# A hybrid RWKV-7 and neighbourhood-attention trunk on one core: the first norm given priority, chunk products over one head's 64 rows, and a load buffer of its own for the decay exponents

## The chip, the cores and the metric

The kernel runs on one core of a Trainium2 chip. The metric is the device time of one execution in microseconds. A core has a matrix engine (PE, with its weight loads shown as PEld), a vector engine (DVE), a scalar engine (ACT), a general engine (POOL) and queues that issue DMAs; most loads here are issued by the queue SP, in order.

## The reference

Two layers are applied to 512 latent tokens and 128 prompt tokens of width 1024 in float32. Every sub-layer starts with a root-mean-square norm and a modulation (shift, scale, gate) made from the conditioning vector; layer 0 mixes tokens with a bidirectional delta-rule recurrence of 16 heads of 64, layer 1 with neighbourhood attention, and each is followed by a squared-ReLU MLP of width 4096. The recurrence is, per head and direction:

```
sa    = S @ (-kk_t)
S_new = S * w_t + sa (kk_t * a_t)^T + v_t k_t^T
y_t   = S_new @ r_t        # w_t = exp(-exp(-softplus(-z) - 0.5))
```

Outputs are both token streams, the final scan states of the prompt, and the prompt's attention keys and values.

## The kernel before, in words

The prompt and the latent tokens are one array of 640 columns, features on the 128 partitions. Instructions are placed by a list scheduler: it simulates a time line of all engines, and each engine then runs its own list in the fixed order that came out; a block under `high_priority` is preferred when several instructions are ready. Within the scan the order on PE is pinned by hand to the order of the program (`mm`).

*Front* (`start_norm`, `rms_bcast`). Four DMAs load the tokens, one the first low-rank weight (`w0[0]`), then 16 DMAs of 512 KB the modulation weights, through six buffers. ACT squares eight tiles (line 331), DVE adds them (336), PE sums over partitions (359), DVE takes an inverse root, five diagonal tiles and five products (381) spread it over the partitions, ACT copies it out, and DVE multiplies the eight token tiles (441). Each quarter of the modulation is produced by PE (286, 296) and added up by DVE (300); ACT then makes the normed tiles `hp` (454), and DVE the token differences `dl` (457 to 460). POOL multiplies `w0[0]` into `w0[1]` (478). The projections follow. Their weight buffers lie where the token tile was.

*Scan.* Tokens are cut into 5 tiles of 128 and these into chunks of 32; two directions run against each other. For each step of tiles, eight units (head group, direction, half) are prepared. `prep_elem` does the elementwise part, once for two units (a pair): it loads the decay exponents (`wi`, line 910, 128x520), `ld_d` (912) and `ld_s` (914), sums the exponents by a scan on DVE (916), takes two exponentials on ACT (917, 918), copies the end factors (`FC`, 920) and makes the scaled keys `KB` (932, 933) on POOL. Then for each unit it takes a free tile C, sets to zero the half of the rows that belongs to the other head, once by a memset on POOL (942) and once by an activation with scale 0 on ACT (939), and writes four scaled products (947, POOL). `prep_group` makes the chunk products of `KB` and C on PE (`pp`, 128 rows by 64 columns, 128 columns streamed): the rows that are not the head's are zero in C. The second 64 columns streamed are the identity kept in C. ACT copies the results (972, 974), and DVE masks one part back into C (977), into the half that held the zeros.

`invert` (984 to 998) solves a 32x32 triangular system for all chunks of a step by some 120 small instructions on DVE. `chain_step` then runs the recurrence over four pairs of chunks: state products (PE, `A`), `U` from the inverse (needs the inversion), the update of the state in bank `B` by 64x64 products at two positions of the array (`state_update`), and `Y`. Between its pieces `fill` prepares units of the next steps; `m_i` and `e_i` count how far the products and the elementwise part have come, and C tiles return to the list `free` after every second chunk. `GU` tiles take the values by DMA (1018). The first preparations run beside the V projection (`tm_product`, 239), whose 20 outputs call `fill` too.

Of the kernel before, what the change touches and what calls it, by code (L numbers as in the profile page):

```python
# [8 lines left out]
F32 = mybir.dt.float32  # L9
F32R = mybir.dt.float32r  # L10
I32 = mybir.dt.int32
AF = mybir.ActivationFunctionType
ALU = mybir.AluOpType
# [3 lines left out]
P = 128  # L17
# [4 lines left out]
T = TS + TP  # L22
# [150 lines left out]
class K:  # L173
# [152 lines left out]
    def rms_bcast(self, x, pool):  # L326
        nc = self.nc
        acc = None
        for k in range(KT):
            sq = pool.tile([P, T], F32, name="sq")  # L330
            nc.scalar.activation(sq, x[:, k, :], AF.Square)
            if acc is None:
                acc = sq
            else:
                n = pool.tile([P, T], F32, name="sqa")
                nc.vector.tensor_tensor(n, acc, sq, op=ALU.add)
                acc = n
        return self.rms_second(self.rms_first(acc, pool), pool)

    def ssq(self, k):  # L340

# [83 lines left out]
    def start_norm(self, st, hp, dl, w0):  # L425

        nc = self.nc
        p2 = self.pool(st, "n1", 2)
        adp = self.pool(st, "adp", 6)
        ps2 = self.pool(st, "n1p", 4, space=PSUM)  # L430
        xt = p2.tile([P, KT, T], F32, name="xt", bufs=1)
        xv = self.A["xT"].rearrange("(k p) t -> p k t", p=P)
        for k2 in range(4):
            nc.sync.dma_start(xt[:, 2 * k2:2 * k2 + 2, :], xv[:, 2 * k2:2 * k2 + 2, :])
        nc.sync.dma_start(w0[0], self.A["lora1"][0])
        self.ada_prepare(p2)
        nc.vector.memset(hp[:, :, 0:1], 0.0)
        nc.vector.memset(hp[:, :, T + 1:T + 2], 0.0)
        rb = self.rms_bcast(xt, p2)
        for k in range(KT):  # L440
            nc.vector.tensor_tensor(xt[:, k, :], xt[:, k, :], rb, op=ALU.mult)
        gs = self.const.tile([P, 8, 2], F32, name="gs00")
        m = self.mods[0]
        for j in range(4):
            for b in (4 + j, j):
                ps = ps2.tile([P, 512], F32, name="adp")
                self.ada_second(*self.ada_first(0, b, adp, ps[:, :256]), ps[:, 256:260])
            ks = slice(2 * j, 2 * j + 2)
            nc.vector.scalar_tensor_tensor(gs[:, ks], m[:, 8 + 2 * j:10 + 2 * j], 1.0,
                                           self.par("norm_g")[:, ks].unsqueeze(2).broadcast_to([P, 2, 2]),  # L450
                                           op0=ALU.add, op1=ALU.mult)
            for k in range(2 * j, 2 * j + 2):
                for a, c, i in ((0, TS, 0), (TS, TP, 1)):
                    nc.scalar.activation(hp[:, k, a + 1:a + 1 + c], xt[:, k, a:a + c], AF.Identity, scale=gs[:, k, i:i + 1],
                                         bias=m[:, k, i:i + 1])
                s = p2.tile([P, T], F32, name="n_s")
                nc.vector.tensor_tensor(s, hp[:, k, 0:T], hp[:, k, 2:T + 2], op=ALU.add)

                nc.vector.tensor_copy(s[:, TS - 1:TS + 1], hp[:, k, TS - 1:TS + 3:3])
                nc.vector.scalar_tensor_tensor(dl[:, k], s, 0.5, hp[:, k, 1:T + 1], op0=ALU.mult, op1=ALU.subtract)  # L460
# [266 lines left out]

    def c_slots(self, pool, n, par):

        for i in range(n):  # L730
            c = pool.tile([P, 26, 64], F32, name=f"C{i}")
            self.nc.any.tensor_copy(c[:, 16:18, :].rearrange("p a x -> p (a x)"), self.cst("ident"))
            self.free[par].append(c)

    def scan_pools(self, st):
# [147 lines left out]
    def fill(self, n):  # L883

        for i in range(n + 1):
# [8 lines left out]
            if self.m_g == 2:  # L894
                self.m_g = 0
                self.m_i += 1
                if self.m_i % 8 == 0:
                    self.invert(u[0])

    def prep_elem(self, ts, hg, d, i):  # L900

        nc = self.nc
        if "FC" not in ts:
            ts["FC"] = self.fcp.tile([P, 2, 2, 2, 4], F32, name="FC")
        ww = (i, 1 - i)[d]
        tt = ts["tiles"][d]
        rev = (lambda a: a[:, :, :, ::-1]) if d else (lambda a: a)
        if i == 0:
            wi = self.el.tile([P, 520], F32, name="wi")
            nc.sync.dma_start(wi, self.tz_d[d][tt, :, hg])  # L910
            dd = self.ld.tile([P, 1024], F32, name="ld_d")
            nc.sync.dma_start(dd, self.dd_d[d][tt, :, hg])
            sh = self.ld.tile([P, 1024], F32, name="ld_s")
            nc.sync.dma_start(sh, self.sh_d[tt, :, hg])
            w = self.el.tile([P, 520], F32, name="w")
            nc.vector.tensor_tensor_scan(wi, self.cst("scan1"), wi, 0.0, ALU.mult, ALU.add)
            nc.scalar.activation(w, wi, AF.Exp, scale=-0.5 * EXPM)
            nc.scalar.activation(wi, wi, AF.Exp, scale=0.5 * EXPM)
            w, wi = (a.rearrange("p (q w t) -> p q w t", w=2, t=65) for a in (w, wi))
            nc.gpsimd.tensor_copy(ts["FC"][:, d, :, :, 2 * hg:2 * hg + 2].rearrange("p w b l -> p l b w"),  # L920
                                  w[:, :, :, 64].rearrange("p (l b) w -> p l b w", b=2))
            self.pe_in = w, wi, dd, sh
        w, wi, dd, sh = self.pe_in
        ex = lambda a, x: a[:, :, x, 0:64].rearrange("p q (e t) -> p q e t", e=2)
        inc = lambda a, x: a[:, :, x, 1:65].rearrange("p q (e t) -> p q e t", e=2)
        v4 = lambda a, j, x: a[:, 512 * j:512 * j + 512].rearrange("p (q w e t) -> p q w e t", q=4, w=2, e=2)[:, :, x]
        if i == 0:
            for j in range(2):
                x = (j, 1 - j)[d]
                f_b, f_k = (inc(wi, x), inc(wi, x)) if d == 0 else (ex(w, x), ex(w, x))  # L930
                KB = ts["KB", hg, d, j] = self.kbp.tile([P, 4, 2, 2, 32], F32, name="KB")
                nc.gpsimd.tensor_tensor(KB[:, :, :, 1], v4(dd, 0, x), f_k, op=ALU.mult)
                nc.gpsimd.tensor_tensor(rev(KB[:, :, :, 0]), v4(dd, 1, x), f_b, op=ALU.mult)
        f_at, f_rt = (ex(w, ww), inc(w, ww)) if d == 0 else (inc(wi, ww), ex(wi, ww))
        C = ts["C"][d, hg, ww] = self.free[ts["par"]].pop(0)
        for h in range(2):
            z = C[64 - 64 * h:P - 64 * h, 8 * h:8 * h + 8, :]
            if h:
                nc.scalar.activation(z.rearrange("p a b -> p (a b)"), self.cst("scan1")[64 - 64 * h:P - 64 * h, :512],
                                     AF.Copy, scale=0.0)  # L940
            else:
                nc.gpsimd.memset(z, 0.0)
        for s, f in ((0, f_at), (1, f_rt)):
            for h in range(2):
                hs = slice(64 * h, 64 * h + 64)
                o = C[hs, 8 * h:8 * h + 8, 32 * s:32 * s + 32].rearrange("p (e q) t -> p q e t", e=2)
                nc.gpsimd.tensor_tensor(rev(o) if s == 0 else o, v4(sh, s, ww)[hs], f[hs], op=ALU.mult)  # L947

    def prep_group(self, ts, hg, d, i, e):

        nc = self.nc
        ww = (i, 1 - i)[d]
        KB, C = ts["KB", hg, d, i], ts["C"][d, hg, ww]
# [3 lines left out]
        pv = pa.rearrange("p (e q x) -> p e q x", e=2, q=4)  # L957
        for q in range(4):
            for h in range(2):
                n = 8 * h + 4 * e + q  # L960
                r = 64 - 64 * h
                self.mm(pv[r:r + 64, e, q, :], lhsT=KB[:, q, e].rearrange("p s t -> p (s t)"), rhs=C[:, n:17 + h:16 + h - n, :],
                        start=True, stop=True, tile_position=(0, r))
        if e == 0:
            return
        if "D" not in ts:
# [2 lines left out]
        pn = pa.rearrange("p (n x) -> p n x", x=P)  # L969
        for h in range(2):  # L970
            for b in range(2):
                nc.scalar.copy(ts["D"][32 * (2 * h + b):32 * (2 * h + b) + 32, d, 4 * hg + 2 * ww:4 * hg + 2 * ww + 2],
                               pv[64 - 64 * h:96 - 64 * h, :, b:4:2, 0:32])
        nc.scalar.copy(C[:, 18:26, :], pn[:, :, 64:P])
        for h in range(2):
            o = slice(64 - 64 * h, P - 64 * h)
            nc.vector.tensor_tensor(C[o, 8 * h:8 * h + 8, :], pn[o, :, 0:64], mask[o], op=ALU.mult)  # L977
# [97 lines left out]
    def state_update(self, ts, n, e, d, gu, nx, C):  # L1075

        nc, tc = self.nc, self.tc
        ee = (3 - e if d else e) % 2
        hs = lambda h: slice(64 * h, 64 * h + 64)
# [3 lines left out]
        if e == 0 and n < 2:  # L1083

            for h in range(2):
                self.mm(G[hs(h)].rearrange("p a b v -> p (a b v)"), lhsT=self.cst("ident")[:, hs(h)],
                        rhs=gu[:, h].rearrange("p a b v -> p (a b v)"), start=True, stop=True,
                        tile_position=(0, 64 * h))
        for pp in range(2):
            for ph in range(4):  # L1090
                for hp in range(2):
                    i = 18 + 4 * ee + 2 * (ph % 2) + pp
                    self.mm(G[hs(hp), pp, ph, :], lhsT=C[ph // 2][ho(hp), i, :], rhs=gu[ho(hp), hp, pp, ph, :],
                            start=False, stop=True, tile_position=(64 - 64 * hp, 64 * hp), skip_group_check=True)
        FC = ts["FC"]
# [507 lines left out]
```

## Time and profile before

| quantity | us |
|---|---|
| median of 3 runs | 2230.84 |
| lowest, highest | 2225.71, 2231.4 |
| profiled execution, its own time | 2227.32 |
| span of the profiled execution | 2225.5 |
| PE busy in it | 2014.0 (90%) |
| DVE busy | 1164.5 (52%) |
| ACT busy | 856.4 (38%) |
| POOL busy | 450.7 (20%) |

The profile is of one execution. Busy times are shares of the span for the whole kernel; they hide that the stages have different limits, so the rows below are by stage. In a row of the time line, the first two numbers are the start and the length in us, then engine, line, operation, output and inputs, and the count of instructions merged; in square brackets stands how long the engine was idle before, and what released it.

### The profile page before, as it was taken

The numbers are of one execution on the slowest core, as the hardware profiler recorded it, in microseconds if no ns is written. First come the engines' busy times: TensorE is split into PE (matmuls) and PEld (weight loads), VectorE is DVE, ScalarE is ACT, GpSimd is POOL, SyncE is SP. The second block draws the span as 40 slices with busy tenths as digits, with TensorE's granted clock in tenths as the row PEclk, the third lists the DMA queues.
The fourth block names the chain that finished last, engine by engine and source line by source line (L and its number), as shares of the span: only waits on it lengthen the run. The fifth ranks groups of instructions, "written<-read, shape, count | busy, mean of one in ns | idle before, by whom it ended". The sixth has DMA issues, their size and how long they took to land.

```text
span 2225.5 us, 44926 instructions
## 1 busy us (share of the span) xinstructions
PE 2014.0 (90%) x18604; PEld 1834.1 (82%) x18604; DVE 1164.5 (52%) x2598; ACT 856.4 (38%) x1712; POOL 450.7 (20%) x547
## 2 busy tenths in 40 slices
PE   5999988757665689999999999999999999999999
PEld 3777777646554579999999998889678999999999
DVE  6655668396688765433333335433666543334342
ACT  4444554445553434313131323221676331313140
POOL 0001276556552201101010110000232110101010
PEclk9997989878888699999999999999999999999999
DMA  6455764544433374223232223433311232222221
GB/s 244 148 162 148 231 203 141 161 129 151 139 126 119 96 219 164 87 77 105 76 107 74 95 76 111 141 130 97 117 44 39 76 114 76 76 77 76 76 76 67
DMA packets 161036, 260.02 MB, mean 117 GB/s; under 512 B 46528, under 2 KB 102976, under 8 KB 160832
## 3 DMA queue, kind: packets, MB, share of 16 engines
q1 hardware_dynamic: 154528, 245.62, 35.3%
q10 hardware_dynamic: 6304, 11.53, 1.5%
q8 instruction: 146, 2.39, 0.4%
q14 instruction: 58, 0.48, 0.1%
HBM read 218.18 MB, written 37.35 MB: 115 GB/s over the span
## 4 chain that ended last, share of the span: by engine, by line
PE 73%; DVE 13%; DMA 5%; POOL 3%; issue 3%; ACT 2%; SPq 1%; DVEq 0%; ACTq 0%; POOLq 0%
PE psl L205 55%; PE psl L239 3%; DVE invX L996 2%; DVE invT L993 2%; PE ps L1530 2%; PE po L1567 2%; POOL C L947 2%; PE pt L1555 2%; PE pp L852 1%; DVE C L977 1%; DMA wi<-scr 1%; PE psl L286 1%; PE st L565 1%; PE pk L698 1%; PE A L852 1%
## 5 line engine op out<-in xcount | busy, mean ns | idle before, releaser
L191 ACT CAST whi<-wraw 128x1024 fp32r<-128x1024 f32 x178 | 186.5, 1049 | 730.5 <-PE psl L205 703.3
L205 PE MATMUL psl<-xh,whi 128*128 128x320 f32 (+1 forms) x1696 | 415.2, 318 | 8.1 <-ACT xh L247 4.9
L205 PE MATMUL psl<-xl,whi 128*128 128x320 f32 (+1 forms) x1696 | 411.0, 315 | 1.5 <-DVE xl L248 1.3
L205 PE MATMUL psl<-xh,wlo 128*128 128x320 f32 (+1 forms) x1696 | 410.1, 314 | 0.4 <-DVE ta L592 0.4
L205 PEld LDWEIGHTS psl<-xh,whi 128*128 128x128 f32 x1696 | 291.9, 192 | 27.0 <-issue 8.6
L205 PEld LDWEIGHTS psl<-xl,whi 128*128 128x128 f32 x1696 | 293.0, 192 | 6.2 <-issue 3.2
L205 PEld LDWEIGHTS psl<-xh,wlo 128*128 128x128 f32 x1696 | 292.9, 191 | 2.9 <-issue 1.7
L1172 DVE SCALAR_TENSOR_TENSOR xres<-psl,mods,xres 128x320 f32<-128x320 f32 (+2 forms) x216 | 81.7, 434 | 305.4 <-PE psl L205 305.4
L1350 POOL TENSOR_TENSOR relu<-relu 128x640 f32<-128x640 f32 x64 | 80.1, 1254 | 765.7 <-ACT relu L1349 750.6
L205 PE MATMUL psl<-hhh,wlo 128*128 128x320 f32 x1024 | 233.2, 309 | 0.0
L205 PE MATMUL psl<-hhl,whi 128*128 128x320 f32 x1024 | 233.2, 309 | 0.0
L205 PE MATMUL psl<-hhh,whi 128*128 128x320 f32 x1024 | 233.2, 309 | 0.0
L193 DVE TENSOR_TENSOR wlo<-wraw,whi 128x1024 fp32r<-128x1024 f32 x178 | 218.5, 1229 | 10.1 <-ACT whi L191 9.7
L205 PEld LDWEIGHTS psl<-hhh,whi 128*128 128x128 f32 x1024 | 170.9, 188 | 0.4 <-issue 0.4
L205 PEld LDWEIGHTS psl<-hhl,whi 128*128 128x128 f32 x1024 | 171.0, 188 | 0.0
L205 PEld LDWEIGHTS psl<-hhh,wlo 128*128 128x128 f32 x1024 | 170.8, 188 | 0.0
L852 PE MATMUL pp<-C,KB 128*64 128x128 f32 x1280 | 102.1, 311 | 42.6 <-DVE C L977 20.0
L1307 DVE TENSOR_TENSOR relu<-psl,rms_b 128x320 f32<-128x320 f32 x128 | 60.8, 486 | 144.4 <-PE psl L205 143.7
L852 PEld LDWEIGHTS pp<-C,KB 128*64 128x64 f32 x1280 | 85.2, 157 | 55.3 <-issue 32.1
L248 DVE TENSOR_TENSOR hhl<-relu,hhh 128x640 fp32r<-128x640 f32 x64 | 53.4, 834 | 127.8 <-ACT hhh L247 127.6
L1052 ACT ACTIVATE GU<-A 32x256 f32<-32x256 f32 x160 | 59.9, 374 | 95.1 <-DVE mods L300 64.7
L852 PE MATMUL A<-GU,C 128*32 128x64 f32 x2560 | 59.0, 246 | 37.9 <-DVE Y L1067 18.3
(305 smaller groups left out, 3389.0 us busy)
## 6 DMA issues: line engine op xcount, KB each, us to landing
wraw<-in_mlp_w SPq DMA_DIRECT2D x128, 512.0 KB, 3.5
adaraw<-in_ada_w SPq DMA_DIRECT2D x96, 512.0 KB, 4.9
ld_d<-scr SPq DMA_DIRECT2D x20, 512.0 KB, 4.2
ld_s<-scr SPq DMA_DIRECT2D x20, 512.0 KB, 3.9
bias<-in_bias SPq DMA_DIRECT2D x16, 384.0 KB, 3.6
scr<-ta SPq DMA_DIRECT2D x16, 325.0 KB, 3.9
wi<-scr SPq DMA_DIRECT2D x20, 260.0 KB, 4.4
scr<-bp SPq DMA_DIRECT2D x16, 320.0 KB, 4.5
```

Of the source, the lines that this page charges most:

```text
L191: nc.scalar.copy(hi, raw)
L193: nc.vector.tensor_tensor(lo, raw, hi.bitcast(F32), op=ALU.subtract)
L205: self.nc.tensor.matmul(ps[g][:, :e - c], lhsT=a[:, k, :], rhs=b[:, c:e], start=(k == 0 and j == 0), stop=(k == n - 1 and j == 2))
L239: nc.tensor.matmul(ps, lhsT=a[:, tc_], rhs=w, start=(k == 0 and j == 0), stop=(k == KT - 1 and j == 2))
L248: (lo_eng or nc.vector).tensor_tensor(xl, src, xh.bitcast(F32), op=ALU.subtract)
L852: r = (op or self.nc.tensor.matmul)(*a, **k)
L947: nc.gpsimd.tensor_tensor(rev(o) if s == 0 else o, v4(sh, s, ww)[hs], f[hs], op=ALU.mult)
L993: nc.vector.tensor_tensor(t, X[:, s + 1:, s:s + 1].broadcast_to([P, m, b - a]), X[:, s:s + 1, a:b].broadcast_to([P, m, b - a]), op=ALU.mult)
L1052: nc.scalar.activation(gu[64 - 64 * hp:96 - 64 * hp, hp, pp].rearrange("p b v -> p (b v)"), U[32 * q:32 * q + 32, :], AF.Copy, scale=-0.5)
L1172: nc.vector.scalar_tensor_tensor(out[:, a:b], ps[g][:, o:o + b - a], gate[:, k, j:j + 1], x[:, a:b], op0=ALU.mult, op1=ALU.add)
L1307: nc.vector.tensor_tensor(t[:, c], ps[q][:, :HALF], rb[:, c], op=ALU.mult)
L1350: nc.gpsimd.tensor_tensor(t, t, t, op=ALU.mult)
```

## The change

In `rms_bcast` the square tiles get eight buffers and the rest of the norm runs under high priority. The load of `w0[0]` moves from behind the tokens to behind the second quarter of the modulation. C loses its zeros and one of its two identity columns: the chunk products run over the 64 rows of their own head, at the array positions (64h, 64-64h). The exponents are loaded into one buffer `tz`, and the load for the pair after is issued right behind the scan that has read it.

```diff
-            sq = pool.tile([P, T], F32, name="sq")
+            sq = pool.tile([P, T], F32, name="sq", bufs=8)
...
-        return self.rms_second(self.rms_first(acc, pool), pool)
+        with self.tc.high_priority():
+            return self.rms_second(self.rms_first(acc, pool), pool)
...
-        nc.sync.dma_start(w0[0], self.A["lora1"][0])
         self.ada_prepare(p2)
...
+            if j == 1:
+                nc.sync.dma_start(w0[0], self.A["lora1"][0])
...
+        ident = self.cst("ident")
         for i in range(n):
-            c = pool.tile([P, 26, 64], F32, name=f"C{i}")
-            self.nc.any.tensor_copy(c[:, 16:18, :].rearrange("p a x -> p (a x)"), self.cst("ident"))
+            c = pool.tile([P, 25, 64], F32, name=f"C{i}")
+            self.nc.vector.tensor_tensor(c[:, 16], ident[:, :64], ident[:, 64:], op=ALU.add)
...
+    def load_tz(self, n=0):
+
+        ts, hg, d, _ = self.units[self.e_i + n]
+        self.tz = self.el.tile([P, 520], F32, name="tz", bufs=1)
+        self.nc.sync.dma_start(self.tz, self.tz_d[d][ts["tiles"][d], :, hg])
...
+            if self.e_i == 0:
+                self.load_tz()
             wi = self.el.tile([P, 520], F32, name="wi")
-            nc.sync.dma_start(wi, self.tz_d[d][tt, :, hg])
...
-            nc.vector.tensor_tensor_scan(wi, self.cst("scan1"), wi, 0.0, ALU.mult, ALU.add)
+            nc.vector.tensor_tensor_scan(wi, self.cst("scan1"), self.tz, 0.0, ALU.mult, ALU.add)
+            if self.e_i + 2 < len(self.units):
+                self.load_tz(2)
...
-        for h in range(2):
-            z = C[64 - 64 * h:P - 64 * h, 8 * h:8 * h + 8, :]
-            if h:
-                nc.scalar.activation(z.rearrange("p a b -> p (a b)"), self.cst("scan1")[64 - 64 * h:P - 64 * h, :512],
-                                     AF.Copy, scale=0.0)
-            else:
-                nc.gpsimd.memset(z, 0.0)
...
-                self.mm(pv[r:r + 64, e, q, :], lhsT=KB[:, q, e].rearrange("p s t -> p (s t)"), rhs=C[:, n:17 + h:16 + h - n, :],
-                        start=True, stop=True, tile_position=(0, r))
+                hs = slice(64 * h, 64 * h + 64)
+                self.mm(pv[r:r + 64, e, q, :], lhsT=KB[hs, q, e].rearrange("p s t -> p (s t)"), rhs=C[hs, n:17:16 - n, :],
+                        start=True, stop=True, tile_position=(64 * h, r))
...
-        nc.scalar.copy(C[:, 18:26, :], pn[:, :, 64:P])
+        nc.scalar.copy(C[:, 17:25, :], pn[:, :, 64:P])
...
-                    i = 18 + 4 * ee + 2 * (ph % 2) + pp
+                    i = 17 + 4 * ee + 2 * (ph % 2) + pp
```

## Rows read from the trace of the kernel before

**Rows 1.** Stretches: length, busy PE, PEld, DVE, ACT, POOL, clock, DMA.
```profile
0.00:29.80 29.80, 12.02 (x111) 7.38 (x112) 12.52 (x40) 9.29 (x16) 2.57 (x5) 1.00 0.91 334
29.80:64.00 34.20, 28.07 (x146) 18.21 (x138) 33.54 (x56) 19.54 (x33) 0.00 (x0) 0.90 0.47 152
...
287.30:401.40 114.10, 98.19 (x869) 89.43 (x867) 75.84 (x162) 53.32 (x129) 72.59 (x99) 0.91 0.53 162
401.40:442.60 41.20, 29.61 (x721) 22.59 (x720) 11.29 (x19) 23.07 (x61) 30.53 (x47) 0.88 0.60 183
442.60:497.40 54.80, 27.63 (x680) 23.50 (x680) 52.48 (x138) 26.03 (x64) 33.57 (x46) 0.74 0.45 140
497.40:528.20 30.80, 27.74 (x623) 21.51 (x625) 9.79 (x25) 18.79 (x51) 15.35 (x22) 0.85 0.38 126
...
840.00:2225.50 1385.50, 1368.65 (x9692) 1294.20 (x9690) 593.15 (x1326) 459.85 (x840) 153.36 (x174) 0.99 0.28 89
```

**Rows 2.** Time line of the front, several engines.
```profile
11.45 0.83 DVE L336 TENSOR_TENSOR sqa<-sqa,sq 128x640 f32<-128x640 f32 x1 [0.33 <-ACT sq L331]
...
12.53 4.18 DVE L336 TENSOR_TENSOR sqa<-sqa,sq 128x640 f32<-128x640 f32 x3
...
13.66 2.36 POOL L478 TENSOR_TENSOR w<-w,parsb 128x1024 f32<-128x1024 f32 x1 [13.22 <-DMA w<-in_lora]
...
21.31 0.17 DVE L264 SCALAR_TENSOR_TENSOR rms_r<-rsq_t,rsq_i 128x5 f32<-128x5 f32 x1
...
28.94 0.49 PE L381 MATMUL psl<-rms_d,cstsb 128*128 128x128 f32 x2
...
29.77 5.97 DVE L441 TENSOR_TENSOR xt<-xt,rms_b 128x640 f32<-128x640 f32 x8 [1.83 <-ACT rms_b L383]
...
37.42 0.64 PE L286 MATMUL adp<-adaraw,condp 128*32 128x256 f32 x8 [0.16 <-DMA adaraw<-in_ada_w]
...
42.50 2.29 ACT L454 ACTIVATE hp<-xt,mods,gs 128x512 f32<-128x512 f32 x4 [1.83 <-DVE mods L300]
...
44.81 1.20 SPq L551 DMA_DIRECT2D wraw<-in_lora  x2
```

**Rows 3.** Instructions on tile C: count, shortest/median/longest in ns, first and last start.
```profile
L852 PE MATMUL pp<-C,KB x1280: 272/273/477, 301.9 to 679.6; 128*64 128x128 f32 x183
...
L942 POOL MEMSET C<- x40: 518/523/538, 284.2 to 660.9; 64x512 f32 x40
L939 ACT ACTIVATE C<-cstsb x40: 612/628/636, 288.8 to 658.3; 64x512 f32<-64x512 f32 x40
```

**Rows 4.** Time line of PE, a chunk product and a state update.
```profile
514.44 1.09 PE L852 MATMUL pp<-C,KB 128*64 128x128 f32 x16
...
518.07 1.15 PE L852 MATMUL B<-GU,C 64*64 64x64 f32 x32
```

**Rows 5.** Zeroing of C by stretch: length, busy (POOL twice, then ACT), clock, DMA.
```profile
287.30:401.40 114.10, 4.42 (x9) 0.91 0.53 162
...
497.40:528.20 30.80, 1.05 (x2) 0.85 0.38 126
...
497.40:528.20 30.80, 1.26 (x2) 0.85 0.38 126
```

**Rows 6.** Waits of PE in 287.3 to 401.4: sum, times, longest.
```profile
PE pp L852 <- POOL C L947: 7.8, 5, 2.3
```

**Rows 7.** Time line of PE inside a chunk product.
```profile
523.51 3.19 PE L852 MATMUL pp<-C,KB 128*64 128x128 f32 x28 [2.21 <-issue]
```

**Rows 8.** Time line around one exponent load, SP, DVE, ACT and PE.
```profile
424.06 1.43 SPq L910 DMA_DIRECT2D wi<-scr  x1
...
428.73 1.24 DVE L916 TENSOR_TENSOR_SCAN wi<-cstsb,wi 128x520 f32<-128x520 f32 x1 [7.49 <-DMA wi<-scr]
...
430.01 0.64 ACT L917 ACTIVATE w<-wi 128x520 f32<-128x520 f32 x1 [8.24 <-DVE wi L916]
...
430.96 1.08 PE L852 MATMUL A<-GU,C 128*32 128x64 f32 x32 [5.44 <-ACT Y L1069]
```

## The prediction

> **What bounds the kernel now.** I read first the busy time by stage, then the chain of waits, then the order of time on each engine around the lines of the diff. By stage [rows 1] there are three kinds of stretch. From 840 us to the end PE is busy 1368.65 of 1385.50 us: nothing in the diff is there, so it only moves as a block. The scan alternates: between the end of one inversion and the start of the next (401.4 to 442.6, 497.4 to 528.2, and two more like these) DVE is busy only 9.8 to 11.3 us, and PE, ACT and POOL hand small pieces to each other; during an inversion (442.6 to 497.4, and three more) DVE is busy 52.48 of 54.80 us and nothing else counts. The stage before the scan (287.3 to 401.4) has PE at 98 and POOL at 73 of 114 us. At the front, DVE is busy 33.54 of 34.20 us from 29.8 to 64. So removed work pays only in the latency stretches, in the V product's stage and at the start; in an inversion it pays nothing.
>
> **The first norm.** The sum of squares ends late: the last three additions take 4.18 us, where one alone takes 0.83, because POOL's multiply of the first low-rank weight (2.36 us) lies on them [rows 2]. That multiply goes later with its load, so the sum ends about 4.18 - 3 x 0.83 = 1.7 us earlier. The rsqrt chain ends at 21.5 [rows 2], so then at 19.8. After it come five diagonal tiles, five products and two copies. They end at 29.7 now, since the last product stands on PE behind modulation products that wait for their weights, and starts at 28.94 [rows 2]. The work itself is small: at 0.49 us for two products [rows 2], with the diagonals between them and the two copies, I estimate 3 us. With priority the norm is ready near 22.8, and DVE, which waited 1.83 us for it before 29.77, starts up to 7.0 us earlier. How much of that stays? The modulation's last weights still arrive by DMA near 37.4, the last shifted tile is made by ACT from 42.50 to 44.79 after waiting for that modulation, and the next weight loads on SP start at 44.81, on that release [rows 2]. The same bytes cross the DMA, so only the waiting inside ACT's queue (the last activations stand behind earlier ones that will be done sooner) and DVE's backlog shrink. Bounds: nothing gained (all is hidden by the last modulation load) or 7.0 us; against it, POOL's multiply now falls beside the eight multiplications of the norm and may cost there the 1.7 us it cost before. I take **-4 us**, the middle, and keep -7 to +1.7. Eight square tiles instead of two only take away ACT's waits for a free tile, inside this. The moved load also moves on SP: behind it stand the last modulation loads, each 512 KB as it is, so one place is exchanged for another and I cost it at nothing; its reader on PE first runs after 41 us.
>
> **Zeros and half-height products.** Gone are 40 POOL memsets at 0.523 us and 40 ACT fills at 0.628 us [rows 3], 20.9 and 25.1 us of engine time. The products stay 1280 of 128 columns; only their height halves. Do they get faster or slower? The state product on B already runs on the same two 64x64 positions, two at a time, into one bank: 32 of 64 columns in 1.15 us, 0.56 ns a column, against 16 of 128 columns in 1.09 us, 0.53 ns a column, for the 128-row form [rows 4]. So I take no change. A 64-row product alone is in no row; the ends are half of today's 68 ns (1.09 us / 16), which would give PE 128 x 34 ns = 4.4 us in a stretch like 497.4 to 528.2 that holds 128 of them, and double, which is rival (d). The Trainium skill (TensorEngine Tiling (Array Packing), Restrictions and Gotchas) speaks against this edit: different row tiles may not use one PSUM bank at the same time. By that rule the two halves would run one after the other and every pair would take twice as long; the trace of the B products, same positions and same bank, disagrees, so the sum goes without it. The identity is built by one DVE addition for each of 16 tiles in place of a copy on whichever engine was free: an exchange of small pieces, nothing, and at worst one addition ahead of the first mask.
>
> What the memsets are worth, by stretch [rows 5]: nine lie in the V stage (4.42 us), and I count eight, 4.2 us, as the first falls before POOL has a tile to make. PE's waits there on POOL's tiles are 7.8 us in five places [rows 6], and PE is what ends that stage: after the last chunk product only V products run, up to 401.4. The gain is at least 0 (the V product's own casts may end last) and at most 7.8; I take **-4.5 us** (4.2 and a little from earlier exponents). In the later stretches between inversions two or three memsets stand in POOL's order ahead of the tiles (1.05 us in 497.4 to 528.2) and two ACT fills (1.26 us) ahead of the copies that DVE's masking waits for; PE then stands 2.21 us at 523.51 in the middle of a chunk product [rows 7]. Three such stretches at 1.5 us, between 0 and 2.7: **-4.5 us** (0 to -8). Inside the inversions they are hidden by DVE: 0.
>
> **The exponents' own buffer.** Today the load goes into the tile that the scan and the exponentials also use, and SP issues it in line, behind the load of ld_s. At 424.06 this is plain [rows 8]: the load lands at 428.7 after DVE has stood 7.49 us, ACT stands 8.24 us for the exponential, and the copy of Y behind it in ACT's queue releases PE 5.44 us late. With its own tile the load follows the scan of the pair before, that is tens of us earlier in this stretch. What is late next is ld_d and ld_s of the same pair, which have as far to come as this load (4.7 us from issue to the scan), but only POOL waits for those, and it has other tiles to make. So ACT's block goes, and of PE's 5.44 us I take **-4 us** (bounds 0 and -5.4). In the other latency stretches the copy that follows in DVE's queue is itself late on ACT, so I add nothing. What is added: 20 loads as before, but each waits for the scan that empties the single buffer, and the next scan waits for it; on SP stand behind it ld_d, ld_s and the GU loads of the chain. Where two scans follow each other closer than the 4.7 us of a load, as the first two pairs may, the second is later than today: at most those 4.7 us once, inside the bound of 0 for the V stage.
>
> **Sum.** -4 - 4.5 - 4.5 - 4 = -17 us, against the profiled execution of 2227.3 us (span 2225.5 us and 1.8 around it): 2210. The median of the three runs is 3.5 us above the profiled one, so a median of new runs stands at 2210 to 2214; I say **2212**. The parts' ends add to -28 and, with the multiply's +1.7, to about +2.
>
> **Rivals.**
> (a) *Hidden anyway.* The front is held by the modulation's DMA, and the inversions, whose length does not change, absorb what POOL gains because their start hangs on PE's pinned order: then only one or two of the four parts arrive, 3 to 9 us, about 2223. For it: DVE's 52 of 55 us in an inversion; against it, the stretches between are not DVE's.
> (b) *More than the parts.* Every stretch also loses the wait of DVE's mask on ACT, since fills and late exponentials leave ACT's queue together; 3 to 4 us more in each of four stretches gives 2197. For it: ACT is busy 18.8 of 30.8 us there. Against it: PE is busy 27.7 of 30.8, so there is little to close.
> (c) *SP's queue blocks: slower.* The exponent load waits on SP for a scan that stands in DVE's queue behind inversion work, and the GU loads behind it come late to the chain. A block of the size seen in [rows 8], 5.4 us on PE, in each of four steps costs 21.6 us; the other parts still give 13, so 2236. It decides from three such blocks on (13 / 5.4). For it: one buffer and one queue in order. Against it: the scheduler places the load where it thinks the scan is done, and SP is blocked in line already today.
> (d) *The two halves serialize*, as the tiling rule would have it. Each product then takes 68 ns more; 128 of them in each of four stretches cost 8.7 us, 35 us in all, and the 869 - 480 = 389 of the V stage (its 4 x 5 x 24 = 480 V products taken from PE's count) up to 26 us: +61 less the 17 of the other parts is about 2271. The page is the tiling one named above; the B rows speak against it.
> That the change does not do what it says (products still of 128 rows, or the norm not first) would show as (a).
>
> **Chances and range.** Forecast 0.55; (a) 0.18; (b) 0.12; (c) 0.11; (d) 0.04. A measurement of this kernel tells a difference of about 0.3% (6.7 us) from no change. Of (a) a third counts as faster, and the low end of the forecast's own case (a gain under 7 us) is small: faster 0.73, same 0.14, slower 0.13. The forecast's own range is 2200 to 2222; to leave out no more than two in ten I go to 2190 on (b)'s side and 2230 on the other, which takes in (a) and the sum of the bad ends.
>
> **What would show it.** After: no memset or fill of C; chunk products as 64x64 with 16 in about 1.1 us (if 2.2, (d)). The eight multiplications of the norm start at 23 to 26 instead of 29.8, the first product after the front 3 to 6 us earlier; if DVE starts early but that product does not, the modulation load held it. The first chain product moves from 401.4 by the front's gain and 4.5 more. DVE's idle before the exponent scans (7.49 us at one) is gone, and SP shows no long wait on a scan with GU loads behind it; if it does, (c). The inversion that now fills 442.6 to 497.4 keeps its 55 us, and 840 to the end keeps 1385. Wrong would be: the first chain product no earlier than 395, or stretches between inversions as long as now.

## The result, and the profile after

The changed kernel takes 2239.62 us (median of 5 runs, 2237.01 to 2241.61) against 2226.68 for the kernel before in the same session: a ratio of 1.0062, 95% interval 1.0046 to 1.0078. It is about 13 us slower, where 17 us faster were forecast. Its profiled execution took 2240.47 us at a span of 2238.7. Of all executions of the runs below one, of the kernel with front and own buffer, took 2803.39 us at a mean granted clock of 0.643 and is left out of that run's ratio.

The stretches of the kernel after, in the columns of [rows 1], cut where the same work begins and ends:

```profile
0.00:26.50 26.50, 12.08 (x104) 7.32 (x108) 12.10 (x40) 9.14 (x16) 2.11 (x5) 1.00 0.95 367
26.50:60.40 33.90, 29.92 (x147) 19.01 (x139) 31.53 (x54) 17.59 (x30) 0.00 (x0) 0.80 0.44 145
275.10:390.20 115.10, 98.11 (x869) 89.52 (x867) 76.02 (x171) 45.66 (x108) 70.32 (x90) 0.88 0.53 162
390.20:435.95 45.75, 31.78 (x721) 23.02 (x720) 9.81 (x17) 20.03 (x54) 26.13 (x39) 0.81 0.54 162
435.95:475.80 39.85, 21.71 (x490) 17.59 (x480) 38.87 (x118) 15.61 (x41) 16.32 (x21) 0.81 0.34 102
475.80:523.35 47.55, 35.73 (x860) 27.35 (x860) 20.75 (x44) 25.31 (x67) 29.53 (x41) 0.87 0.51 162
```

Read against [rows 1], the front ends earlier (29.80 became 26.50), and the V product's stage keeps its length (114.10 became 115.10) although nine memsets left it. Then the scan has another shape: the inversion shrank from 54.80 to 39.85 us, and the stretch behind it grew from 30.80 to 47.55. PE's instructions moved from the one to the other: 680 and 623 before, 490 and 860 now. By end points, the last product of the projections came 12.3 us earlier (287.4 to 275.1), the last V product 11.2 earlier, the last product of the scan's output projection 10.5 later (862.2 to 872.7). So 21.7 us were lost between the last two, and some 3 behind them (the stretch from there to the last product takes about 1358 or about 1361 us in kernels with and without each edit, so that is not the change).

The front in the time line after, answering [rows 2]. POOL's multiply now lies behind the sum of squares, and the eight multiplications start at 26.48 instead of 29.77:

```profile
21.30 1.90 POOL L480 TENSOR_TENSOR w<-w,parsb 128x1024 f32<-128x1024 f32 x1 [20.86 <-DMA w<-in_lora]
...
25.65 0.49 PE L382 MATMUL psl<-rms_d,cstsb 128*128 128x128 f32 x2
...
26.48 2.30 DVE L441 TENSOR_TENSOR xt<-xt,rms_b 128x640 f32<-128x640 f32 x3 [0.86 <-ACT rms_b L384]
```

The chunk products on tile C after, answering [rows 3], and 16 of them in the time line, answering [rows 4]. They have half the height, and neither their spacing (16 in 1.09 us) nor their duration changed by more than 4 ns; no memset and no fill is left on C:

```profile
L855 PE MATMUL pp<-C,KB x1280: 266/269/473, 291.1 to 689.4; 64*64 64x128 f32 x183
```

```profile
511.28 1.09 PE L855 MATMUL pp<-C,KB 64*64 64x128 f32 x16
```

What is late in the scan shows in PE's waits from the first chain product to the output projection, first before (401.4 to 831.3), then after (390.2 to 840.4); columns: sum in us, times, longest.

```profile
PE A L852 <- DVE rsq_t L262: 17.5, 1, 17.5
PE A L852 <- DVE TT L998: 14.3, 2, 13.0
PE A L852 <- ACT Rc L1035: 12.1, 13, 2.5
...
PE A L852 <- ACT Y L1069: 5.4, 1, 5.4
PE A L852 <- ACT GU L1052: 4.6, 2, 2.9
PE B L852 <- ACT GU L1052: 4.4, 6, 1.4
```

```profile
PE B L855 <- ACT GU L1058: 30.9, 11, 9.2
PE A L855 <- ACT Rc L1041: 24.3, 16, 5.2
...
PE A L855 <- ACT GU L1058: 12.7, 4, 6.8
```

The chain's copies on ACT (`Rc`, `GU`, `Y`) held PE for 26.5 us before and for 67.9 now. That is not the net loss. The first two rows are waits for an inversion to end (the one put down to `rsq_t` ends at 497.60, just behind the last transpose of the inversion); these 31.8 us are gone after, when no inversion is waited for. All rows of PE's waits in the two windows add to 136 us before and 152 after. The longest wait for a copy, in the time line after, on POOL, DVE, ACT and PE:

```profile
406.13 5.88 POOL L952 TENSOR_TENSOR C<-ld_s,wi 64x256 f32<-64x256 f32 x8 [1.84 <-DMA ld_s<-scr]
...
412.04 1.24 DVE L926 TENSOR_TENSOR_SCAN wi<-cstsb,tz 128x520 f32<-128x520 f32 x1 [8.04 <-POOL C L952]
...
413.31 0.64 ACT L929 ACTIVATE w<-wi 128x520 f32<-128x520 f32 x1 [10.47 <-DVE wi L926]
...
416.06 1.55 ACT L1058 ACTIVATE GU<-A 32x256 f32<-32x256 f32 x4
...
417.26 2.37 PE L855 MATMUL B<-GU,cstsb 128*64 128x512 f32 x4 [9.24 <-ACT GU L1058]
```

ACT's list has the exponential ahead of the chain's `GU`. The exponential waits for the scan, the scan for a free `wi`, and that is released when POOL has made its tiles: `GU`, which needs none of this, leaves 9.24 us late.

Not every late copy is of this kind. The second longest wait, later in the same time line:

```profile
551.75 0.15 DVE L300 TENSOR_TENSOR mods<-A,parsb 128x4 f32<-128x4 f32 x1
...
551.93 1.57 ACT L1058 ACTIVATE GU<-A 32x256 f32<-32x256 f32 x4 [13.01 <-DVE mods L300]
...
552.36 2.37 PE L855 MATMUL B<-GU,C 64*64 64x64 f32 x32 [7.98 <-ACT GU L1058]
```

Here `GU` waits for DVE: the sums for a later modulation lie in the same tile `A` as what `GU` copies, and DVE's list has the small addition that reads them (`mods`) among the steps of the inversion. Of the waits of 1 us and more on a copy, 30.5 us (six places) stand behind an exponential that had waited, and 12.9 us (four places) on a `mods`; before, 6.8 us (two places) and none.

### The profile page after: what moved, and what is told of

It reads as the page before. It is cut to its first block, busy times and chain, and to the rows that moved or that the text cites. A ratio compares the mean times of both kernels' runs of the same rounds, so it can differ in the third digit from the quotient of the medians.

```text
span 2238.7 us, 44845 instructions
## 1 busy us (share of the span) xinstructions
PE 2019.3 (90%) x18604; PEld 1832.4 (82%) x18604; DVE 1153.9 (52%) x2608; ACT 834.9 (37%) x1662; POOL 427.1 (19%) x507
## 4 chain that ended last, share of the span: by engine, by line
PE 71%; DVE 10%; DMA 6%; issue 5%; POOL 4%; ACT 2%; SPq 1%; ACTq 0%; DVEq 0%; POOLq 0%
PE psl L205 53%; PE psl L239 4%; POOL C L952 3%; PE ps L1536 2%; DVE invT L999 2%; DVE invX L1002 2%; PE po L1573 2%; PE pt L1561 2%; PE pp L855 1%; DMA adaraw<-in_ada_w 1%; PE psl L286 1%; PE pk L700 1%; DVE C L983 1%; PE A L855 1%; DMA ld_s<-scr 1%
## 5 line engine op out<-in xcount | busy, mean ns | idle before, releaser
L855 PE MATMUL pp<-C,KB 64*64 64x128 f32 x1280 | 99.6, 303 | 25.1 <-DVE C L983 12.7
L855 PEld LDWEIGHTS pp<-C,KB 64*64 64x64 f32 x1280 | 82.2, 151 | 38.7 <-issue 20.0
L983 DVE TENSOR_TENSOR C<-pp,cstsb 64x512 f32<-64x512 f32 x80 | 55.1, 689 | 104.4 <-ACT C L980 96.3
```

Source lines behind the costliest of these rows:

```text
L855: r = (op or self.nc.tensor.matmul)(*a, **k)
```

## The experiments

The first theory (T1) was that the own buffer does this, since its early load lets the scan and the exponentials be placed early. Four runs took the change apart. Unless said, a ratio is to the kernel before on the same chip.

**The own buffer alone.**

```diff
+            if self.e_i == 0:
+                self.load_tz()
...
+            nc.vector.tensor_tensor_scan(wi, self.cst("scan1"), self.tz, 0.0, ALU.mult, ALU.add)
+            if self.e_i + 2 < len(self.units):
+                self.load_tz(2)
```

> The kernel before with the exponents' own buffer as its only change: the load is issued behind the scan that empties the buffer, one pair ahead; zeros, 128-row products and the front as before. Theory T1 (the early load lets the scan on DVE and the exponentials on ACT be placed earlier in their fixed queues, where they then really wait for w and wi and for the inversion, and ACT's Rc, GU and Y for the chain stand behind them): the whole loss comes from here, the scan from the first chain product to the projections behind it becomes 15 to 25 us longer, time 2240 to 2252. Rival T2 (the reordering comes from the missing zeros and the 64-row products): within 7 us of before, 2220 to 2234. Rival T4 (any edit to the scan reshuffles the fixed queues by some 10 us in either direction): no prediction of sign, and each part alone moves by 5 to 15 us.

Measured 2228.14 against 2226.5, ratio 1.0010 (0.9994 to 1.0026). T1 falls, and so does the prediction's 4 us: by itself the buffer does nothing. T4 wanted a move of 5 us or more from each part, and falls with it.

**64-row products without zeros, alone.**

```diff
-        for h in range(2):
-            z = C[64 - 64 * h:P - 64 * h, 8 * h:8 * h + 8, :]
...
+                self.mm(pv[r:r + 64, e, q, :], lhsT=KB[hs, q, e].rearrange("p s t -> p (s t)"), rhs=C[hs, n:17:16 - n, :],
+                        start=True, stop=True, tile_position=(64 * h, r))
```

> The kernel before with 64-row chunk products, no zeros and the 25-column C as its only change; exponent load and front as before. T1: no loss, what the prediction gave the zeros, 4 to 9 us, arrives: 2217 to 2223. T2: the scan becomes 10 to 20 us longer, 2237 to 2247. T4: somewhere between 2212 and 2242.

Measured 2272.93, ratio 1.0219 (1.0196 to 1.0243): 46 us slower, more than twice what the rival gave it.

**The front alone.**

```diff
+        with self.tc.high_priority():
+            return self.rms_second(self.rms_first(acc, pool), pool)
...
+            if j == 1:
+                nc.sync.dma_start(w0[0], self.A["lora1"][0])
```

> The kernel before with eight square tiles, the norm under high priority and the later load of the first low-rank weight as its only change; the scan as before. The trace of the changed kernel shows the last g product 12.3 us earlier, of which 3.3 us are there at the norm's multiply and 9.7 us appear between 63 and 287 us. T1: the front keeps its gain through the scan: 2213 to 2220, and if the 9.7 us come from the projections' order and not from the clock, the nearer to 2213. Rival T3 (the front moves the placement of everything behind it and costs the scan what it gained): 2225 to 2240. T4: the last g product is not earlier by more than 4 us.

Measured 2221.44, ratio 0.9977 (0.9959 to 0.9995): 5 us faster, 1.4 us above what T1 gave it. Its last product of the projections came at 278.4, 9.0 us before that of [rows 1]'s kernel, but only part of that is the edit: see the last section.

**All but the own buffer.**

```diff
+            nc.sync.dma_start(wi, self.tz_d[d][tt, :, hg])
...
-            if self.e_i + 2 < len(self.units):
-                self.load_tz(2)
```

> The changed kernel without the exponents' own buffer: the load goes back into the tile that the scan uses, in its old place; the norm's priority, the 64-row products and the missing zeros stay. T1: the changed kernel's loss is gone and front and zeros give 12 to 20 us together: 2207 to 2215. T2: still slow, 2230 to 2240. T3: slow as well, and the run with the front alone is slow too. T4: between the two, not the sum of the runs with one part.

Measured 2262.88, ratio 1.0169 (1.0146 to 1.0192). Slow, as T2 says, and slower than T2's range. The own buffer therefore saves 23 us beside the 64-row products, and nothing beside the 128-row ones. Without it the chain's copies hold PE for 92.7 us instead of 67.9, and the waits of 1 us and more behind an exponential are 60.2 us instead of 30.5.

Which half of the edit is it, the form of the products or the missing zeros?

**64-row products, zeros kept.**

```diff
+                hs = slice(64 * h, 64 * h + 64)
+                self.mm(pv[r:r + 64, e, q, :], lhsT=KB[hs, q, e].rearrange("p s t -> p (s t)"), rhs=C[hs, n:17 + h:16 + h - n, :],
+                        start=True, stop=True, tile_position=(64 * h, r))
```

> The kernel before with the 64-row chunk products alone: C keeps its zeros, its 26 columns and its identity, exponent load and front as before. The run with all of this edit took 2272.9 us against 2226.5. Theory F (the form of the products does it: it changes where the scheduler places the other engines' work): 2260 to 2285, inversions of 37 to 44 us with some 50 us between them. Rival Z (the missing zeros do it, since a fill on ACT or POOL no longer stands between the steps): 2220 to 2232, inversions of 46 to 53 us as before.

Measured 2274.0, ratio 1.0211 (1.0189 to 1.0234); the second and third inversion take 37.9 and 42.3 us, with 54 behind each. Z falls: the form alone makes the whole loss, with the zeros in place. It issues exactly the instructions of the kernel before, one for one, so the two can be crossed. A few lines at the end of the program pin each engine's scan instructions (933 on DVE, 613 on ACT, 352 on POOL, 355 issues on SP) to a recorded order:

```diff
+    for seq in ORDER:
+        for a, b in zip(seq, seq[1:]):
+            tc.add_manual_dep(ins[f"I-{b}"], f"I-{a}", info, reason="order")
```

**64-row products in the old order** (the diff above on the run above).

> The 64-row products with zeros of the run above, and in the scan the instructions of DVE, ACT, POOL and the DMA queue are pinned to the order that they have in the kernel before, each engine's list by its own (PE's is pinned in both). Theory O (the products cost the same and only the order of the four lists makes the time): 2222 to 2231. Rival P (the 64-row products themselves cost on PE, by the bank that both halves write or by a lower clock): stays above 2250.

Measured 2222.99, ratio 0.9978 (0.9962 to 0.9994).

**128-row products in the new order** (the same lines on the kernel before).

> The crossed case: the kernel before with its 128-row products, its four lists in the scan pinned to the order that the scheduler gave the kernel with 64-row products and zeros. Theory O: slow without any 64-row product, 2260 to 2285. Rival P: 2222 to 2232.

Measured 2267.03, ratio 1.0176 (1.0151 to 1.0201). The four corners:

| median, us | old order | new order |
|---|---|---|
| 128 rows, zeros | 2226.4 | 2267.0 |
| 64 rows, zeros | 2223.0 | 2274.0 |

Going across costs 41 to 51 us with not one instruction changed; going down costs -3 or +7. Theory O holds, P falls. One inversion (up to its last transpose) and the stretch to the next in the columns of [rows 1], before, then in the 64-row kernel with the old order, then in the 128-row kernel with the new:

```profile
442.56:495.53 52.97, 27.63 (x680) 23.50 (x680) 50.64 (x136) 25.22 (x64) 33.37 (x45) 0.75 0.46 145
495.53:528.17 32.64, 27.71 (x622) 21.48 (x624) 11.63 (x25) 19.61 (x53) 15.52 (x23) 0.83 0.36 119
```

```profile
445.55:499.22 53.67, 26.52 (x680) 22.87 (x680) 52.00 (x136) 25.21 (x64) 31.58 (x45) 0.75 0.46 144
499.22:529.99 30.77, 27.26 (x684) 21.00 (x688) 11.62 (x25) 19.64 (x53) 15.83 (x23) 0.88 0.39 127
```

```profile
452.95:490.92 37.97, 19.46 (x414) 15.11 (x416) 36.54 (x116) 14.63 (x37) 15.75 (x21) 0.78 0.32 100
490.92:546.50 55.58, 38.92 (x878) 31.11 (x876) 24.07 (x46) 30.92 (x79) 32.44 (x48) 0.81 0.44 143
```

The first two kernels agree to 2 us in both stretches; the third, with the products of the first, has the shape of the changed kernel. In the old order DVE runs 20 more instructions inside the inversion (136 against 116: masks, updates of the chain's `Y`, `GU` and `B`, pieces of the output norm; the inversion's own hundred small steps are the same), and 266 more of PE's lie beside it. In the new order the inversion is 15 us shorter, and the stretch behind it 23 longer. There PE waits for ACT, in PE's waits of the 128-row kernel with the new order (404 to 871.9), and in its time line:

```profile
PE A L852 <- ACT Rc L1035: 48.0, 16, 10.8
PE B L852 <- ACT GU L1052: 22.8, 9, 14.0
...
PE A L852 <- ACT GU L1052: 13.2, 4, 6.6
...
PE A L852 <- ACT GU L1108: 0.3, 1, 0.3
```

```profile
430.71 1.24 DVE L916 TENSOR_TENSOR_SCAN wi<-cstsb,wi 128x520 f32<-128x520 f32 x1 [13.97 <-DMA wi<-scr]
...
431.99 0.64 ACT L917 ACTIVATE w<-wi 128x520 f32<-128x520 f32 x1 [14.14 <-DVE wi L916]
...
432.65 1.55 ACT L1052 ACTIVATE GU<-A 32x256 f32<-32x256 f32 x4
...
433.85 2.37 PE L852 MATMUL B<-GU,cstsb 128*64 128x512 f32 x4 [14.02 <-ACT GU L1052]
```

This is the block of [rows 8], grown: 84.3 us of PE's waits on the chain's copies, against 26.5 before and 27.7 in the 64-row kernel with the old order (the sums of such rows); 53 of the 84 are waits of 1 us and more behind an exponential that had waited. Here the exponential stands ahead of `GU` with no own buffer, and waits 14.14 us, since the load itself is late; with the buffer (the changed kernel, above) 10.47. Together with the 60.2 and 30.5 us above, that is how the own buffer pays in the new order and not in the old.

**128-row products without zeros.** The kernel leaves out the masked part of the chunk products, which is multiplied by zeros.

```diff
+            self.nc.any.memset(c[:, 0:16, :].rearrange("p a x -> p (a x)"), 0.0)
...
-                nc.gpsimd.memset(z, 0.0)
...
+            nc.vector.tensor_tensor(C[o, 8 * h:8 * h + 8, :], pn[o, :, 0:64], zero[o], op=ALU.mult)
```

> The kernel before with 128-row products, but the zeros of C are written only once, when the 16 tiles are made; so that they stay zero, the masked part written back into them is multiplied by zeros (the part of the chunk products that comes through the mask is left out of the result). Theory F: order of before, and the 40 memsets and 40 fills gone are worth what the prediction gave them, 0 to 9 us: 2217 to 2228. Rival Z: 2260 to 2285.

Measured 2240.97, ratio 1.0059 (1.0037 to 1.0081). Neither theory: inversions keep 42 to 56 us, yet it is 15 us slower; 10 of them lie behind the last inversion (from its end to the last product of the output projection 146.7 us against 136.2). The lists were not compared here; that missing zeros move them too is likely, not shown.

**No zeros, 64 rows, old order.**

> The kernel before with 64-row products and without the zeros of C (the 40 memsets and 40 fills), the rest of the four lists in the scan pinned to the order of the kernel before. It prices the zeros with the order held still; 64-row products with zeros in the old order took 2223.0. Theory W (the prediction's terms: 4.5 us in the V stage and 4.5 us after it): 2212 to 2217. Rival N (POOL and ACT have the time to spare, the zeros were hidden): 2220 to 2226.

Measured 2229.03 against 2225.43, ratio 1.0012 (0.9995 to 1.0029). W falls, and the time lies 3 us above N's range too: with the order held, 80 instructions less gain nothing, and against the 64-row kernel with zeros (0.9978) the time is 6 to 8 us longer, for which no cause was found. PE's waits on POOL's C tiles in the V stage, 7.8 us in five places in [rows 6], are 9.0 in six here: what POOL lacks there is not the time of the memsets.

**Front and own buffer, 128 rows and zeros kept** (the first and third diffs of this section).

> The front edits and the exponents' own buffer together, 128-row products and zeros as before, no order pinned beside that of PE. Alone the front took 2221.4 and the buffer 2228.1 against 2226.5. Theory A (the parts add up as long as the scheduler keeps its order): 2220 to 2225. Rival R (every pair of edits reshuffles the lists): outside 2215 to 2230.

Measured 2219.79 against 2225.43 (2218.78 without the one long execution), ratio 0.9968 (0.9951 to 0.9984): 1 us below A's range, and R falls. It is the front's gain, and the fastest ratio of all runs, though its interval overlaps with those of 0.9977, 0.9978 and 0.9981.

**The changed kernel in the old order.** The whole change, its four lists pinned to those of the run above.

> The changed kernel, whole, with its four lists in the scan pinned to the order that the scheduler gives the run above (front edits and own buffer, 128-row products), less the zeros. Theory O (only the order cost the changed kernel its time): 2207 to 2222, at the low end if the zeros pay as predicted, at the high end if they were hidden. Rival P (something else in the changed scan is slow, for instance the exponent's load behind its scan): 2230 to 2242.

Measured 2220.76, ratio 0.9981 (0.9963 to 0.9998), as O says, at its high end. The changed kernel becomes faster than the kernel before; its order alone cost it the difference, 1.0062 to 0.9981, or 18 us. PE's waits on the chain's copies fall from 67.9 to 34.0.

**The same without the own buffer.**

> As the run above but without the exponents' own buffer: front edits, 64-row products, no zeros, the lists pinned to the order of the kernel with the front edits alone. Natural order took 2262.9. Theory O: 2208 to 2221, and the difference from the run above is what the own buffer is worth with the order held (the prediction: 4 us in its favour; rival: nothing or a loss of 2). Rival P: above 2240.

Measured 2228.51, ratio 1.0004 (0.9984 to 1.0024). Neither theory: above O's range, below P's. It is the one held order that lost the front's gain, by a V stage of 123.3 us (280.2 to 403.5) where the run above has 112.9. POOL stands 15.4 us there for loads of `ld_s` (11.5 at one place; 7.2 in the run above), and the granted clock is 0.85 instead of 0.91; which of the two comes first is open. Read as the expectation asked, the own buffer is worth 5 to 8 us here.

Two last runs asked which of the lists it is.

**Only DVE's list old.**

> The changed kernel with only DVE's list in the scan pinned to the order of the kernel with the front edits and the own buffer; ACT, POOL and the DMA queue as the scheduler then places them. The changed kernel took 2239.6, with all four lists pinned 2220.8. Theory D (the loss is on DVE: its new list runs an inversion almost without the masks and copies of the chain, so that PE's products stand after it instead of beside it): 2217 to 2226. Rival Q (ACT's exponentials ahead of the chain's Rc, GU and Y make the loss, as first thought): 2232 to 2242.

Measured 2228.93 against 2228.33, ratio 0.9998 (0.9986 to 1.0011).

**Only ACT's, POOL's and SP's lists old.**

> The complement: the changed kernel with the lists of ACT, POOL and the DMA queue pinned to that older order, DVE's free. Theory D: 2232 to 2250, since DVE's list stays as it is in the changed kernel. Rival Q: 2217 to 2226.

Measured 2231.16, ratio 1.0019 (1.0005 to 1.0034). Of the 0.81% between the changed kernel's order and the old one, DVE's list recovers 0.64 and the others 0.43: neither theory, both carry the loss and share a part of it. With DVE's list old the inversion holds 680 of PE's instructions again (56.76 us, 32.49 behind it) and PE's waits on the chain's copies are 44.5 us; with the others old the inversion stays bare (37.20, then 48.27), and those waits are 47.6. What remains differs in kind. With DVE's list old, no wait of 1 us or more on a copy is on a `mods`, and 23.9 us stand behind exponentials; with the others old, 13.1 us are on a `mods` and 4.8 behind an exponential. So DVE's list brings the one kind of block and ACT's the other.

## Why the prediction was wrong, point by point

- **The step that failed** is "So I take no change" for the half-height products, and with it the inversion that "keeps its 55 us": a change of the lists was put at nothing. The step was right of the products (269 ns against 273, 16 in 1.09 us) and wrong of the kernel: without the zeros they cost 46 us, and of the whole change the order alone makes 18 us. The durations were read from a trace whose lists were taken as given; but the lists are made anew from every edit, and this one moved masks and chain updates out of the inversions, put exponentials ahead of the chain's copies on ACT, and made some of these copies wait for a `mods` on DVE. Why the scheduler did so is inferred only: fewer of PE's instructions beside an inversion is what comes out if it reckons 64-row products as longer than they are. The trace does not hold its reckoning.
- **The sum** would have failed without this too: with the order held the whole change gains 4 us, not 17.
- **The first norm**, -4 us: measured -5.0. The multiplications came 3.3 us earlier, inside the 7.0 given but just behind the 23 to 26 us that the test named, the first product of the projections 2.6 earlier, a little under the 3 to 6 written.
- **Zeros**, -9 us: no gain with the order held (6 to 8 us lost against the 64-row kernel that has them), and a loss of 15 with the order free. The V stage, which was to be 4.5 us shorter, kept its length. The 7.8 us of [rows 6] were taken for memsets in POOL's way; they stayed when these went.
- **Own buffer**, -4 us: 0 beside the 128-row products; 5 to 8 us between the two kernels with all lists old, which lie in a V stage whose length is open. The stall of [rows 8] was real, but taking its load away alone did not move the end: DVE now waits 13.0 us before the scans for a free `wi`, where it waited 30.4 for the loads.
- **Rival (c)** named 2236, near the result, by another mechanism: a load that waits for a scan. Its sign did show: SP stands up to 12.9 us with an exponent load that waits for DVE inside an inversion. Its price did not: PE waits 1.0 us in all for the `GU` loads behind, and the scans wait 4.0 us for their own. That the number is near is luck. The place was right to look at, for the exponential behind the scan is a part of what blocks; the lists that block are ACT's and DVE's, not SP's.
- **Rival (d)** falls: the spacing of the products did not double. That says nothing about the rule it took up. At a granted clock of 1.00 in all these places, products over the whole array, with 320 columns, come two every 0.29 us in the kernel before, 0.45 ns a column:

```profile
899.83 0.45 PE L205 MATMUL psl<-xh,whi 128*128 128x320 f32 x2
900.12 0.46 PE L205 MATMUL psl<-xl,whi 128*128 128x320 f32 x2
```

The chunk products take 0.53 ns a column, before and after, and those on B 0.56 [rows 4]: neither is faster than one product behind the other. So the prediction's "two at a time" is not shown by its rows, and there was no overlap to lose. By the Trainium skill (TensorEngine Tiling (Array Packing), Restrictions and Gotchas) different row tiles may not use one PSUM bank at once; no run here shows whether two of these products ever do.

- **The tests it set**: inversions were said to keep 55 us, and lost 15; the first chain product came at 390.2, earlier than 395, and still the kernel was slower, because that test ended where the loss began. The other sign of being wrong came true: the stretches between inversions are longer than before (45.75 and 47.55 us against 41.20 and 30.80).

## What to carry to other kernels

Where a scheduler makes fixed lists from its own reckoning, an edit's price is its instructions plus what it does to the lists, and here the second was the larger (41 us and more, against 3 and 7). Before trusting a sum read from the old trace, compare the order of the new lists with the old around each long block, above all how many instructions of the critical chain still stand inside it; then pin the old order once, so that the edit and the order are timed apart. An instruction that waits long and for another stage should not stand ahead of the chain's copies on an engine that runs its list in order, nor a small result that they wait for behind a long block on another.

## What the runs showed of the hardware

Of this kind one thing was not expected: the granted clock in a stage that does the same work differs between kernels, and flatters one profile against another. Columns as in [rows 1]; the same 40 us of the projections, and the rest of that stage, before and after:

```profile
160.00:200.00 40.00, 36.79 (x134) 29.46 (x135) 29.65 (x45) 19.23 (x36) 3.14 (x2) 0.62 0.31 90
200.00:287.80 87.80, 80.87 (x498) 69.08 (x496) 58.17 (x74) 43.34 (x75) 25.49 (x18) 0.92 0.77 231
```

```profile
157.00:197.00 40.00, 33.55 (x165) 26.53 (x166) 33.52 (x50) 23.08 (x42) 3.10 (x2) 0.87 0.37 110
197.00:275.60 78.60, 72.66 (x465) 62.81 (x464) 55.62 (x71) 40.99 (x72) 24.04 (x14) 0.96 0.83 248
```

At 0.62 against 0.87 PE gets 134 products done where the other gets 165, and the two stretches together are 9.2 us shorter. In both the clock falls from 2.4 to 1.2 GHz near 162 us, behind 4 us in which PE was busy for only 1.26 (before) and 1.55 (after); it stands at 0.50 in every slice of 4 us from 164 to 192 before, and only from 161 to 169 after. The same 40 us, counted from the norm's multiplications, have a share of 0.57 to 0.70 in the eight kernels without the front edits, and of 0.59 to 0.87 in the eight with them: 0.70 with the front alone, 0.87 in the changed kernel. Whether that follows from the order of the instructions there was not tested. The start moves too: the norm's multiplications begin at 29.8 to 30.4 or at 32.6 to 33.4 in kernels without the front edits, at 26.5 to 26.7 or 30.0 to 30.7 with them. Only medians of several runs say that the front is worth 5 us, not 12.
